# The FFN down projection as seven block products instead of eight, with weight sums added up in DRAM

## The chip, the cores and the metric

The kernel runs on one core of a Trainium2 chip. A core has five engines with a queue of instructions each, taken in order: TensorE (PE in the rows, its weight loads PEld), VectorE (DVE), ScalarE (ACT), GpSimd (POOL) and SyncE (SP, which here only issues DMAs). They wait for one another through semaphores. DMAs are issued by SP, ACT and POOL and are carried out by 16 DMA engines. The metric is the device time of one execution, in microseconds (us), as the median of several runs.

## The reference

A decoder block on 512 tokens of width 1024, in float32: a gated linear recurrence and a sparse attention side by side, merged, and then a SwiGLU feed-forward block of width 2816. What the change touches is the last line but one:

```python
h = rms_norm(x, norm_ffn_pre[l])
f = (jax.nn.silu(h @ w_ffn_gate[l]) * (h @ w_ffn_up[l])) @ w_ffn_down[l]
x = x + rms_norm(f, norm_ffn_post[l])
```

Here `h` is 512 x 1024, the bracket (called `ff` below) is 512 x 2816, and `w_ffn_down` is 2816 x 1024.

## The kernel before

Every float32 product is made as three matmuls. An operand is split into a rounded part `hi` (written by ScalarE as a cast) and the rest `lo` (written by VectorE as source minus `hi`), and the product is hi x hi + hi x lo + lo x hi. `split` (L83 to L84) is that pair of instructions, and nearly every operand goes through it.

The stages in order of time: the input projections and the recurrence (to about 245 us), its output projection `rnn_out`, eight units of weights (to about 286), the attention, the merge and `w_o` (to about 540), the FFN's gate and up projections (`columns(m)`, 22 column blocks of 128, to 762), and the down projection with the last norm (762 to 889).

In the attention, 64 units (16 heads by 4 blocks of 128 queries) are run in an order written out by hand: `logits(u)` is made three units ahead (`AHEAD = 3`) of `probs(u)`, and between them run the matmuls of 13 further projections ("fill": queries, keys, gates), whose 512 KB weight tiles are loaded on POOL's queue (L220), multiplied by -1 on ScalarE (L246), and completed by a second, adding DMA on POOL's queue (L247), so that the tile holds `lo`. A query projection also needs a rotary step: ScalarE evacuates, VectorE shuffles (L478), POOL multiplies twice (L479, L480), VectorE adds (L481). TensorE's order is kept as written there; the other engines' orders are chosen by a scheduler when the program is built.

The gate and up projections already use seven block products with sums of blocks. For column block m, VectorE adds up weight blocks for block m + 1 (L971 to L974), splits them, and evacuates seven products (L1007 to L1013).

The down projection before is the plain one. For each of 22 row blocks k of 128, `load_d` brings 512 KB of weights, `prep_d` splits them, `prep_a` splits the matching pair of `ff` blocks every second time, and `down_mm` adds three matmuls (128 x 128 stationary, 512 columns moving) into each of eight PSUM banks, (q, c) for four blocks of 128 tokens and two halves of the output columns. For the last four k (`TAIL`), the order is bank by bank, so that `finish(q)` (the norm, the residual, the store) of one token block runs beside the matmuls of the next. `raw_tile`, `ws_tile` and the tag `tt` are small rotating sets of buffers.

## Time and profile before

| | |
|---|---|
| median of 3 runs | 892.28 us (889.8 to 892.52) |
| profiled execution | 890.67 us, of which the span of its instructions is 888.8 us and 1.87 us lie around it |
| TensorE, VectorE, ScalarE, GpSimd busy, share of the span | 96%, 70%, 56%, 26% |
| mean granted TensorE clock | 0.991 of full speed |

A busy share is a mean over all stages. Matmuls overlap one another in the pipeline: one lasts longer than the distance from its start to the next one's, so a stage's length is read from starts.

### The profile page before, as it was taken

Reading aid. Unit: us, or ns where it says so; the run is one execution under the profiler, and the core shown is the slowest. Engines: PE = TensorE matmul, PEld = TensorE weight load, DVE = VectorE, ACT = ScalarE, POOL = GpSimd, SP = SyncE. Lnnn points to the kernel's source line nnn. Section 1 sums busy time; section 2 is a strip of 40 time slices with the busy share of each in tenths; the row PEclk is TensorE's granted clock in tenths of the full one; section 3 lists DMA queues with packets and bytes.
Section 4 is the critical chain, followed back from the end, with each engine's and each line's share of the span. In section 5 each row is a group of like instructions: output and inputs, shape, how many; then the busy total and the mean of one; then the engine's idle time right before and its main releaser. Section 6 shows DMA issues by size and latency. Waiting matters only on the chain.

```text
span 888.8 us, 12985 instructions
## 1 busy us (share of the span) xinstructions
PE 857.5 (96%) x4811; PEld 740.9 (83%) x4811; DVE 620.6 (70%) x1109; ACT 494.7 (56%) x838; POOL 229.2 (26%) x242
## 2 busy tenths in 40 slices
PE   8999999999899989999999998999999999999996
PEld 5887888877688778888788887899999999888885
DVE  7686989976861687777466379888878887533415
ACT  5355457877430878777534356666656666323312
POOL 3262235453421432210022202233333332100000
PEclk9999999999899999999999999999999999999998
DMA  9488788758344745433445635778788878333104
GB/s 303 105 175 183 164 165 178 162 126 184 96 94 113 166 90 108 100 73 119 147 142 180 210 137 151 172 167 189 174 189 181 182 177 226 110 114 98 48 0 143
DMA packets 65697, 129.73 MB, mean 146 GB/s; under 512 B 8865, under 2 KB 32481, under 8 KB 65634
## 3 DMA queue, kind: packets, MB, share of 16 engines
q0 software_dynamic: 18432, 61.87, 35.6%
q1 hardware_dynamic: 46048, 64.92, 23.4%
q10 hardware_dynamic: 1154, 2.10, 0.6%
q8 instruction: 38, 0.62, 0.3%
q14 instruction: 25, 0.20, 0.1%
HBM read 122.59 MB, written 6.29 MB: 145 GB/s over the span
## 4 chain that ended last, share of the span: by engine, by line
PE 62%; DVE 13%; DMA 8%; issue 8%; ACT 7%; POOL 2%; SPq 0%; DVEq 0%; ACTq 0%; POOLq 0%
PE acc L286 6%; PE acc L284 6%; PE acc L288 6%; PE bank L990 5%; DMA ws<-in_t_ff_dram 5%; PE bank L988 4%; PE bank L989 4%; PE bank L1064 3%; PE bank L1062 3%; PE bank L1063 3%; PE ps_o L742 2%; PE ps_t L732 2%; DVE xc L584 2%; PE acc L990 1%; PE acc L988 1%
## 5 line engine op out<-in xcount | busy, mean ns | idle before, releaser
L84 DVE TENSOR_TENSOR ws<-raw,ws 128x1024 fp32r<-128x1024 f32 x44 | 61.0, 1390 | 66.2 <-ACT ws L84 66.2
L284 PE MATMUL acc<-hT,ws 128*128 128x512 f32 x248 | 98.7, 398 | 1.4 <-ACT xpad L580 1.4
L286 PE MATMUL acc<-hT,ws 128*128 128x512 f32 x248 | 99.0, 399 | 0.0
L288 PE MATMUL acc<-hT,ws 128*128 128x512 f32 x248 | 98.7, 398 | 0.0
L84 ACT CAST ws<-raw 128x1024 fp32r<-128x1024 f32 x44 | 46.1, 1052 | 71.0 <-PE bank L1064 37.5
L982 POOL DMA_DIRECT2D ws<-in_t_ff_dram x40 | 35.2, 881 | 157.6 <-ACT ws L981 88.6
L84 ACT CAST ws<-sums 128x1024 fp32r<-128x1024 f32 x40 | 40.1, 1048 | 52.6 <-DVE sums L972 51.7
L990 PE MATMUL bank<-T,ws 128*128 128x256 f32 x200 | 57.8, 290 | 2.0 <-DMA ws<-in_t_ff_dram 1.7
L988 PE MATMUL bank<-T,ws 128*128 128x256 f32 x200 | 56.5, 283 | 1.1 <-ACT ws L84 1.1
L284 PEld LDWEIGHTS acc<-hT,ws 128*128 128x128 f32 x248 | 46.7, 188 | 11.8 <-ACT xpad L580 1.9
L989 PE MATMUL bank<-T,ws 128*128 128x256 f32 x200 | 56.4, 282 | 0.0
L989 PE MATMUL bank<-B,ws 128*128 128x256 f32 x200 | 56.3, 282 | 0.0
L988 PE MATMUL bank<-B,ws 128*128 128x256 f32 x200 | 56.1, 281 | 0.0
L990 PE MATMUL bank<-B,ws 128*128 128x256 f32 x200 | 55.9, 280 | 0.0
L286 PEld LDWEIGHTS acc<-hT,ws 128*128 128x128 f32 x248 | 46.7, 188 | 10.0
L288 PEld LDWEIGHTS acc<-hT,ws 128*128 128x128 f32 x248 | 46.7, 188 | 9.8
L84 DVE TENSOR_TENSOR ws<-sums,ws 128x1024 fp32r<-128x1024 f32 x40 | 48.0, 1238 | 7.5 <-ACT ws L84 7.5
L284 PE MATMUL acc<-hT,raw 128*128 128x512 f32 x120 | 48.0, 400 | 1.2 <-ACT gl L572 1.2
L286 PE MATMUL acc<-hT,raw 128*128 128x512 f32 x120 | 48.1, 401 | 0.0
L288 PE MATMUL acc<-hT,raw 128*128 128x512 f32 x120 | 47.7, 398 | 0.0
L246 ACT ACTIVATE ws<-ws 128x1024 fp32r<-128x1024 f32 x29 | 30.7, 1059 | 23.2 <-DMA ws<-in_t_in_dram 23.2
L973 POOL TENSOR_TENSOR sums<-raw 128x512 f32<-128x512 f32 x20 | 33.5, 1675 | 34.7 <-PE acc L990 10.8
(329 smaller groups left out, 2696.6 us busy)
## 6 DMA issues: line engine op xcount, KB each, us to landing
ws<-in_t_in_dram POOLq DMA_DIRECT2D x58, 512.0 KB, 5.6
raw<-in_t_ff_dram SPq DMA_DIRECT2D x40, 512.0 KB, 4.4
raw<-in_t_in_dram POOLq DMA_DIRECT2D x30, 512.0 KB, 5.6
raw<-in_w_ffn_down_dram SPq DMA_DIRECT2D x22, 512.0 KB, 3.7
ws<-in_t_ff_dram POOLq DMA_DIRECT2D x20, 512.0 KB, 5.7
ws<-in_t_ff_dram POOLq DMA_DIRECT2D x20, 256.0 KB, 6.9
raw<-in_w_rnn_out_dram SPq DMA_DIRECT2D x8, 512.0 KB, 4.2
raw<-in_w_att_out_dram SPq DMA_DIRECT2D x8, 512.0 KB, 4.1
```

The lines of the kernel that those rows point to most:

```text
L84: return SC.copy(hi, src).ins, (lo_engine or V).tensor_tensor(lo, src, f(hi), op=A.subtract).ins
L246: SC.mul(lo, f(hi), -1.0)
L284: pe(PE.matmul(ps, ws[0][:, k, :], hi(k), start=(n == 0), stop=False))
L286: pe(PE.matmul(ps, ws[0][:, k, :], lo(k), start=False, stop=False))
L288: pe(PE.matmul(ps, ws[1][:, k, :], hi(k), start=False, stop=(n == len(order) - 1)))
L973: G.tensor_tensor(s3, a11, a21, op=A.subtract)
L982: G.dma_start(dst[:, 1], t_ff[n, m].rearrange("p (k c) -> p k c", c=P)[:, k], accum_op=A.add)
L988: PE.matmul(ps, a[:, 0, k, :], b[:, 0, k, :], start=(k == 0), stop=False)
L989: PE.matmul(ps, a[:, 0, k, :], b[:, 1, k, :], start=False, stop=False)
L990: PE.matmul(ps, a[:, 1, k, :], b[:, 0, k, :], start=False, stop=(k == 3))
L1062: PE.matmul(ps, a[:, 0, ts], b[:, 0, cs], start=(k == 0), stop=False)
L1063: PE.matmul(ps, a[:, 0, ts], b[:, 1, cs], start=False, stop=False)
```

## The change

The down projection `ff @ w_ffn_down` is written as a 2 x 2 block product and made with seven block products instead of eight. The blocks of `ff` are two halves of the tokens (256 each) by even and odd row blocks; those of the weights are even and odd row blocks by two halves of the output columns (512). With four sums of weight blocks (U1 to U4) and three sums of `ff` blocks, the products are P1 to P7. Each product has 11 steps j (one per pair of row blocks), two token blocks t and three matmuls per step.

The weight sums are made in DRAM. Two new inputs hold copies of weight blocks in another order (`t_dn`, `t_dn2`). `down_sums(n)`, called at two places in `rnn_out`'s loop and at five in the attention, issues for a group of three j (11 j in four groups): first a 1 MB copy within DRAM on SP's queue, at the next call a 512 KB adding DMA on POOL's queue, and at the two calls after that a 256 KB adding DMA each. That is 11 copies on SP's queue and 33 adding DMAs on POOL's, all with source and target in DRAM.

The down projection then has two phases. In the first, P6, P5, P7 and P4 run together over j with the summed weights (1 MB per j): `prep_d` splits them and `prep_a` makes the three `ff` sums on VectorE and splits these and two blocks. In the second, P1, P3 and P2 run one after the other, with weight blocks loaded from `w_ffn_down` itself and `ff` blocks split again (`prep_l`). Then the results are added up on VectorE, and `finish` follows; for the last product the first token block's matmuls stand ahead of the second's (`TAIL = 6` steps).

```diff
+    def down_sums(n):
+        for step, g in enumerate(range(n, n - 4, -1)):
+            for j in range(GROUP * g, min(GROUP * g + GROUP, NJ)) if g >= 0 else ():
+                u = u_dram[j]
+                with tc.issue_after(after["pool"]), tc.issue_after(after["sp"]):
+                    if step == 0:
+                        ld(u, t_dn[j])
+                    elif step == 1:
+                        G.dma_start(u[:, 0:2], t_dn2[j], accum_op=A.add)
+                    else:
+                        G.dma_start(u[:, step:step + 1], u[:, 2 * step - 4:2 * step - 3], accum_op=A.add)
...
         rnn_out(m)
         drain(4)
+        if m in (1, 5):
+            down_sums(m // 4)
...
             values(u // NT - 1)
+            if u // NT % 3 == 2:
+                down_sums(2 + u // NT // 3)
...
+    def prep_d(j):
+        x, z = ws_tile(0, [P, 2, 2, 512]), ws_tile(1, [P, 2, 2, 512])
+        for raw, w in zip(raw_d.pop(j), (x, z)):
+            split(raw, w[:, 0], w[:, 1])
...
+    def prep_a(j):
+        ff = ff_pair(j)
+        a11, a12, a21, a22 = ff[:, 0, 1], ff[:, 1, 1], ff[:, 0, 0], ff[:, 1, 0]
+        sa = ffp.tile([P, 2, H], F32, name="sa", tag="u", bufs=2)
+        V.tensor_tensor(sa[:, 0], a22, a21, op=A.subtract)
+        V.tensor_tensor(sa[:, 1], a11, a21, op=A.subtract)
+        V.scalar_tensor_tensor(a21, sa[:, 0], -1.0, a11, op0=A.mult, op1=A.subtract)
+        t = ws_tile(0, [P, 2, 4, H]) if j == 0 else ffp.tile([P, 2, 4, H], F32R, name="as", tag="tt", bufs=4)
+        split(sa, t[:, 0, 0:2], t[:, 1, 0:2])
+        split(ff[:, :, 0], t[:, 0, 2:4], t[:, 1, 2:4])
...
-    for k in range(FT):
-        if k + 2 < FT:
-            load_d(k + 2)
...
+    for j in range(NJ):
+        if j + 2 < NJ:
+            load_d(j + 2)
+        if j + 1 < NJ:
+            prep_d(j + 1)
+            prep_a(j + 1)
+        wd, ad = ws_d.pop(j), as_d.pop(j)
+        for t in range(2):
+            for n, a, b in (("P6", "S2", "U2"), ("P5", "R1", "U1"), ("P7", "S3", "U3"), ("P4", "A22", "U4")):
+                down_mm(pq[n, t], t, ad[a], wd[b], j == 0, j == NJ - 1)
...
+    jobs = [("P1", 0, 0), ("P3", 1, 1), ("P2", 1, 0)]
+    steps = [(n, e, c, j0) for n, e, c in jobs for j0 in range(0, NJ, 2)]
...
+    for t in range(2):
+        p6, p5, p7, p4 = (pq[n, t] for n in ("P6", "P5", "P7", "P4"))
+        V.tensor_copy(xb[:, 0, t], p6)
+        V.tensor_tensor(xb[:, 1, t], p5, xb[:, 0, t], op=A.add)
+        V.tensor_tensor(xb[:, 0, t], p7, xb[:, 0, t], op=A.add)
+        V.tensor_tensor(xa[:, 1, t], p5, xb[:, 0, t], op=A.add)
+        V.tensor_tensor(xa[:, 0, t], p4, xb[:, 0, t], op=A.add)
...
+    for t in range(2):
+        for i in range(len(steps) - TAIL, len(steps)):
+            step_mm(i, t)
+        V.tensor_tensor(xb[:, 0, t], pl["P2", t], xb[:, 0, t], op=A.add)
+        finish(t, [xb[:, 0, t], xb[:, 1, t]])
```

In the rows below, lines of the change are those of the changed kernel: `split`'s VectorE half is L85 there, loads of fill weights L221, their adding DMAs L248, the rotary products L480 and L481.

First place, POOL's queue in the attention, from the load of one fill weight to the next rotary step. In the kernel before:

```order
L220 DMA ws_3333<-in_t_in_dram 128x1024
L247 DMA raw_3077<-in_t_in_dram 128x1024
L220 DMA raw_3459<-in_t_in_dram 128x1024
L479 TENSOR_TENSOR rp_x_3446<-rp_x_3446,rope_c_131 128x512
L480 TENSOR_TENSOR rp_s_3447<-rp_s_3447,rope_s_132 128x512
```

and in the changed one, of the same stretch, up to the second load (L694 is the 512 KB addition, L696 the 256 KB ones):

```order
L221 DMA ws_3373<-in_t_in_dram 128x1024
L694 DMA u_dram9_1977<-in_t_dn2_dram 128x1024
L694 DMA u_dram10_1978<-in_t_dn2_dram 128x1024
L696 DMA u_dram6_1974<-u_dram6_1974 128x512
L696 DMA u_dram7_1975<-u_dram7_1975 128x512
L696 DMA u_dram8_1976<-u_dram8_1976 128x512
L696 DMA u_dram3_1971<-u_dram3_1971 128x512
L696 DMA u_dram4_1972<-u_dram4_1972 128x512
L696 DMA u_dram5_1973<-u_dram5_1973 128x512
L248 DMA raw_3106<-in_t_in_dram 128x1024
L221 DMA raw_3507<-in_t_in_dram 128x1024
```

Eight adding DMAs now stand between the two loads, and five more (two for group 3, three for group 2) between the second load and the same rotary step. Each DMA on this queue is issued only once the eighth DMA before it on the queue has landed, since they share eight semaphores in turn. The longest row of additions, nine, stands one fill unit earlier.

Second place, VectorE at the end of the gate and up projections. `o`, `u` and `ff<-o` are evacuations of `columns`; `ws<-raw` splits down weights, `sa` and `as` are sums of `ff` blocks and their splits. In the kernel before, between the evacuation of the last but one column block and the last one's:

```order
L1013 TENSOR_TENSOR ff<-o 128x512
L84 TENSOR_TENSOR ws<-raw,ws 128x1024 x2
L1007 TENSOR_TENSOR u<-u 128x256
L1008 TENSOR_TENSOR o<-acc,u 128x512
L1009 TENSOR_TENSOR o<-acc,o 128x256
L84 TENSOR_TENSOR ws<-ff,ws 128x1024
```

and in the changed one, from the same evacuation:

```order
L1035 TENSOR_TENSOR ff<-o 128x512
L85 TENSOR_TENSOR ws<-raw,ws 128x1024 x2
L1090 TENSOR_TENSOR sa<-ff 128x256
L1091 TENSOR_TENSOR sa<-ff 128x256
L1029 TENSOR_TENSOR u<-u 128x256
L1092 SCALAR_TENSOR_TENSOR ff<-sa,ff 128x256
L1030 TENSOR_TENSOR o<-acc,u 128x512
L85 TENSOR_TENSOR ws<-raw,ws 128x1024
L1032 TENSOR_TENSOR o<-bank_7653,u 128x256
L85 TENSOR_TENSOR as<-sa,as 128x512
L1031 TENSOR_TENSOR o<-acc,o 128x256
```

The sums and splits for the first steps of the down projection are interleaved with the last evacuations.

Third place, VectorE at the very end of the changed kernel: `acc_8592` is P2 of the first token block and `acc_8651` that of the second, L1221 adds them, L884 multiplies by the norm's gain, L888 makes the output rows.

```order
L1221 TENSOR_TENSOR xb_8207<-acc_8592,xb_8207 128x512
L884 TENSOR_TENSOR rest_8631<-xb_8207,xc_8208 128x512
L96 TENSOR_SCALAR rs_v_8639<-ss2_8632 128x1
L884 TENSOR_TENSOR rest_8690<-xb_8207,xc_8208 128x512
L99 RECIPROCAL rs_r_8641<-rs_r_8641 128x1
...
L888 SCALAR_TENSOR_TENSOR rest_8631<-rest_8631,rs_r_8641,x1_8629 128x512
L888 SCALAR_TENSOR_TENSOR rest_8631<-rest_8631,rs_r_8641,x1_8627 128x512
L1221 TENSOR_TENSOR xb_8207<-acc_8651,xb_8207 128x512
L884 TENSOR_TENSOR rest_8690<-xb_8207,xc_8208 128x512
```

The addition for the second token block stands behind the first block's whole norm. On TensorE, the scheduler mixes the two blocks' matmuls: 17 of them come after the first block's last one.

## Rows read from the trace of the kernel before

**Rows 1.** The page: part 1, TensorE to GpSimd; part 2, the granted clock.
```profile
PE 857.5 (96%) x4811; PEld 740.9 (83%) x4811; DVE 620.6 (70%) x1109; ACT 494.7 (56%) x838; POOL 229.2 (26%) x242
...
PEclk9999999999899999999999999999999999999998
```

**Rows 2.** Windows: stretch, its length, busy us (x instructions) of PE, PEld, DVE, ACT, POOL, clock, DMA share, GB/s.
```profile
744.50:762.00 17.50, 17.50 (x148) 17.49 (x148) 10.88 (x15) 9.55 (x12) 1.77 (x2) 1.00 0.86 248
762.00:881.80 119.80, 119.73 (x529) 98.79 (x527) 45.35 (x56) 34.52 (x46) 3.16 (x1) 1.00 0.25 78
881.80:888.80 7.00, 0.00 (x0) 0.00 (x0) 2.77 (x7) 0.89 (x3) 0.00 (x0) 0.64 0.20 76
```

**Rows 3.** Timeline of TensorE (start, duration): first and last down matmul; a fill's start.
```profile
294.21 0.48 PE L284 MATMUL acc<-hT,raw 128*128 128x512 f32 x1
...
761.87 0.39 PE L1062 MATMUL bank<-ws 128*128 128x512 f32 x1
...
881.35 0.39 PE L1064 MATMUL bank<-wt,ws 128*128 128x512 f32 x1
```

**Rows 4.** Groups, 762 to 889 us: busy us, mean ns, idle before it and its releaser.
```profile
L84 DVE TENSOR_TENSOR ws<-raw,ws 128x1024 fp32r<-128x1024 f32 x14 | 17.0, 1223 | 37.9 <-ACT ws L84 37.9
L84 ACT CAST ws<-raw 128x1024 fp32r<-128x1024 f32 x14 | 14.6, 1053 | 40.7 <-PE bank L1064 37.5 <-issue 3.2
...
L866 DVE SCALAR_TENSOR_TENSOR rest<-rest,rs_r,x 128x512 f32<-128x512 f32 x8 | 5.7, 749 | 0.1
...
L862 DVE TENSOR_TENSOR rest<-bank,gfin 128x512 f32<-128x512 f32 x6 | 4.1, 689 | 17.1 <-ACT u L109 17.1
```

**Rows 5.** Timeline of VectorE in the evacuation of a column block.
```profile
742.07 0.41 DVE L1010 TENSOR_TENSOR o<-bank,u 128x256 f32<-128x256 f32 x1
742.39 0.68 DVE L1011 TENSOR_TENSOR o<-bank,o 128x512 f32<-128x512 f32 x1
743.77 0.69 DVE L1013 TENSOR_TENSOR ff<-o 128x512 f32<-128x512 f32 x1 [0.70 <-ACT o L1012]
```

**Rows 6.** Timeline at the end: norm of the third and the last token block.
```profile
876.39 0.60 ACT L109 ACTIVATE u<-acc 128x512 f32<-128x512 f32 x1 [2.03 <-PE acc L1064]
...
878.84 1.42 DVE L866 SCALAR_TENSOR_TENSOR rest<-rest,rs_r,x 128x512 f32<-128x512 f32 x2
...
881.83 0.60 ACT L109 ACTIVATE u<-bank 128x512 f32<-128x512 f32 x1 [2.03 <-PE bank L1064]
...
882.55 0.69 DVE L862 TENSOR_TENSOR rest<-bank,gfin 128x512 f32<-128x512 f32 x1 [1.69 <-ACT u L109]
...
884.28 1.42 DVE L866 SCALAR_TENSOR_TENSOR rest<-rest,rs_r,x 128x512 f32<-128x512 f32 x2
```

**Rows 7.** Windows, the attention, columns as in rows 2.
```profile
300.00:400.00 100.00, 97.19 (x541) 83.15 (x540) 79.04 (x205) 80.54 (x195) 27.43 (x29) 1.00 0.48 97
```

**Rows 8.** Timeline of GpSimd, fill weights and a rotary step.
```profile
254.89 0.59 POOL L220 DMA_DIRECT2D raw<-in_t_in_dram  x1 [7.17 <-DVE ws L84]
...
359.70 0.55 POOL L220 DMA_DIRECT2D ws<-in_t_in_dram  x1 [7.47 <-PE acc L288]
...
371.91 1.29 POOL L479 TENSOR_TENSOR rp_x<-rp_x,rope_c 128x512 f32<-128x512 f32 x1 [1.54 <-DVE rp_s L478]
```

**Rows 9.** The page: part 3 (packets, MB, share of 16 engines), part 6 (us to landing).
```profile
q1 hardware_dynamic: 46048, 64.92, 23.4%
...
ws<-in_t_ff_dram POOLq DMA_DIRECT2D x20, 512.0 KB, 5.7
ws<-in_t_ff_dram POOLq DMA_DIRECT2D x20, 256.0 KB, 6.9
```

**Rows 10.** Timeline of VectorE in the attention: the same unit of two heads.
```profile
374.03 0.42 DVE L716 CUSTOM_DVE_ANT_0 sm<-ps_s,mask 128x256 f32<-128x256 f32 x1
...
382.30 0.42 DVE L716 CUSTOM_DVE_ANT_0 sm<-ps_s,mask 128x256 f32<-128x256 f32 x1 [0.59 <-PE ps_s L711]
```

**Rows 11.** Timeline of SyncE's queue: the last five loads for `rnn_out`.
```profile
224.66 24.53 SPq L230 DMA_DIRECT2D raw<-in_w_rnn_out_dram  x5
```

More of the change, by code (lines that the diff above doesn't have):

```diff
@@ L36 @@
 PLAIN = 2
-TAIL = 4
+TAIL = 6
 START = 24
@@ L229, in do_load @@
         if kind == "c":
-            ld(raw, w[:, where:where + P].rearrange("(k p) c -> p k c", p=P))
+            after["sp"] = ld(raw, w[:, where:where + P].rearrange("(k p) c -> p k c", p=P)).ins
         else:
@@ L678, in hybrid_block @@
     gb_dram = dram.tile([KT, P, S], F32, name="gb_dram")
+    NJ = FT // 2
+    u_dram = [dram.tile([P, 4, 512], F32, name=f"u_dram{j}") for j in range(NJ)]
+    def down_sums(n):
[9 more added lines that the diff above has]
+                        G.dma_start(u[:, step:step + 1], u[:, 2 * step - 4:2 * step - 3], accum_op=A.add)
     def gate_b(m):
@@ L1055, in prep_a, with load_d @@
-    def prep_a(j):
-        as_d[j] = ws_tile(1, [P, 2, 2 * S])
-        split(ff_pair(j).rearrange("p e n c -> p (e n c)"), as_d[j][:, 0], as_d[j][:, 1])
-    def down_mm(ps, k, q, c):
-        a, b = as_d[k // 2], ws_d[k]
-        ts, cs = slice(k % 2 * S + q * P, k % 2 * S + (q + 1) * P), slice(c * 512, (c + 1) * 512)
-        PE.matmul(ps, a[:, 0, ts], b[:, 0, cs], start=(k == 0), stop=False)
-        PE.matmul(ps, a[:, 0, ts], b[:, 1, cs], start=False, stop=False)
-        PE.matmul(ps, a[:, 1, ts], b[:, 0, cs], start=False, stop=(k == FT - 1))
+    def load_d(j):
+        raw_d[j] = []
+        for c in range(2):
+            t = raw_tile(c, [P, 2, 512])
+            ld(t, u_dram[j][:, 2 * c:2 * c + 2, :])
+            raw_d[j].append(t)
@@ L1066, in hybrid_block, with down_mm @@
+    def down_mm(ps, t, a, b, first, last):
+        ts = slice(t * P, (t + 1) * P)
+        PE.matmul(ps, a[:, 0, ts], b[:, 0], start=first, stop=False)
+        PE.matmul(ps, a[:, 0, ts], b[:, 1], start=False, stop=False)
+        PE.matmul(ps, a[:, 1, ts], b[:, 0], start=False, stop=last)
+    NJ = FT // 2
     for m in range(PLAIN, FT):
@@ new lines, in hybrid_block, with load_l, prep_l @@
+    raw_l, ws_l, as_l = {}, {}, {}
+    def load_l(i):
+        n, e, c, j0 = steps[i]
+        w = min(2, NJ - j0)
+        raw_l[i] = raw_tile(i % 2, [P, 2, 512])
+        ld(raw_l[i][:, 0:w], w_dn[e][:, j0:j0 + w, c * 512:(c + 1) * 512])
+    def prep_l(i):
+        n, e, c, j0 = steps[i]
+        w = min(2, NJ - j0)
+        x = ws_tile(i % 2, [P, 2, 2, 512])
+        raw = raw_l.pop(i)
+        split(raw[:, 0:w], x[:, 0, 0:w], x[:, 1, 0:w])
+        if i % 2 == 0:
+            as_l[i] = ffp.tile([P, 2, 4, H], F32R, name="al", tag="tt", bufs=4)
+        t = as_l[i - i % 2][:, :, i % 2 * 2:i % 2 * 2 + 2]
+        for q in range(w):
+            ff = ff_pair(j0 + q)
+            a = {"P1": ff[:, 0, 1], "P2": ff[:, 1, 1], "P3": ff[:, 0, 0]}[n]
+            if n == "P3":
+                V.scalar_tensor_tensor(a, ff[:, 1, 1], -1.0, a, op0=A.mult, op1=A.subtract)
+            split(a, t[:, 0, q], t[:, 1, q])
+        ws_l[i] = x, t
@@ L1086, in finish @@
+    for i in range(2):
+        load_l(i)
+    prep_l(0)
+    for t in range(2):
[5 more added lines that the diff above has]
+        V.tensor_tensor(xa[:, 0, t], p4, xb[:, 0, t], op=A.add)
+    def finish(t, cs):
         base = []
@@ L1117, in hybrid_block, with step_mm @@
-    for q in range(NT):
-        for c in range(2):
-            for k in range(FT - TAIL, FT):
-                down_mm(pd[q, c], k, q, c)
-        finish(q)
+    pl = {}
+    def step_mm(i, t):
+        n, e, c, j0 = steps[i]
+        if j0 == 0:
+            pl[n, t] = acc() if n == "P2" else bank4()
+        for q in range(min(2, NJ - j0)):
+            down_mm(pl[n, t], t, ws_l[i][1][:, :, q], ws_l[i][0][:, :, q], j0 + q == 0, j0 + q == NJ - 1)
+    for i, (n, e, c, j0) in enumerate(steps):
+        if i + 2 < len(steps):
+            load_l(i + 2)
+        if i + 1 < len(steps):
+            prep_l(i + 1)
+        if i < len(steps) - TAIL:
+            for t in range(2):
+                step_mm(i, t)
+        if j0 + 2 >= NJ and n == "P1":
+            for t in range(2):
+                SC.copy(xb[:, 0, t], pl["P1", t])
+                V.tensor_tensor(xb[:, 1, t], pl["P1", t], xb[:, 1, t], op=A.add)
+                for q in range(2):
+                    V.tensor_tensor(xa[:, q, t], xa[:, q, t], xb[:, 0, t], op=A.add)
+            for t in range(2):
+                finish(t + 2, [xa[:, 0, t], xa[:, 1, t]])
+        if j0 + 2 >= NJ and n == "P3":
+            for t in range(2):
+                V.tensor_tensor(xb[:, 1, t], pl["P3", t], xb[:, 1, t], op=A.add)
@@ L1166 @@
     named.append(("t_ff", _np.stack([_tiled(inputs[n], range(0, D_FF, P)) for n in ("w_ffn_gate", "w_ffn_up")])))
+    dn = _np.asarray(inputs["w_ffn_down"])[0].reshape(FT // 2, 2, P, 2, 512).transpose(0, 2, 1, 3, 4)
+    blocks = {f"{e + 1}{c + 1}": dn[:, :, e, c] for e in range(2) for c in range(2)}
+    named.append(("t_dn", _np.stack([blocks[n] for n in ("11", "22", "22", "21")], axis=2)))
+    named.append(("t_dn2", _np.stack([blocks["12"], blocks["12"]], axis=2)))
     for name, a in named:
```

56 lines of the change are left out of this document (21 added, 35 removed).

## The prediction

> **What bounds the kernel now.** I read the page first: TensorE is busy for 96% of the span and its clock stays at the upper level, 2.4 GHz, nearly throughout [rows 1]. Then the windows: from 762 to 881.8 us, the down projection, TensorE is busy all the time (119.73 of 119.80), while VectorE works 45 us, ScalarE 35 and the DMA engines are 25% busy [rows 2]. So this stage is bound by the number of matmuls alone, and a matmul less is time less, as long as the other engines keep up. What one costs is not its 0.39 us. The stage's first matmul starts at 761.87 and its last at 881.35 [rows 3], and there are 528 (22 k, 8 banks, 3 each; the window counts 529 with one of the stage before): 119.48 / 527 = 0.2267 us from start to start. After the last, 7 us follow in which TensorE is idle.
>
> **What is removed.** Seven products of 11 j, 2 t and 3 matmuls are 462, all with 512 columns as before: 66 fewer. 66 x 0.2267 = 15.0 us, which the change can gain and not more.
>
> **VectorE in the down projection.** This is where the cover is thin. Before, it had 22 weight splits and 11 `ff` splits; now it has 37 splits of 128x1024 or the like, sums, second splits of `ff`, and additions of products. From the evacuation that ends at 743.77 + 0.69 = 744.5 [rows 5], counted along the order to the last weight split of the last step, there stand 37 instructions of 1024 elements, 53 of 512, 83 of 256 and 6 tiny ones (six evacuations of 512 and six of 256 of the last two column blocks among them). By durations of 1.22, 0.69, 0.42 and 0.2 us [rows 4, 5] that is 45.1 + 36.6 + 34.9 + 1.2 = 117.8 us. But instructions that don't wait start before the one ahead has ended: 742.07 to 742.39 is 0.32, where the duration is 0.41 [rows 5]. At 0.08 less for each of 173 it is 104 us. TensorE reaches that split's product at its 444th matmul, 761.87 + 443 x 0.2267 = 862.3, so VectorE has 117.8 us for it. By durations the room is zero, by starts it is 13.8 us, a load of 88%. The room can't be used freely: the buffers let VectorE run about three steps ahead in the first phase, where a step costs it 2 x 1.14 + 2 x 0.61 + 4 x 0.34 = 4.9 us against TensorE's 24 x 0.2267 = 5.4; and each `lo` waits for ScalarE's cast, which comes in ScalarE's own order. ScalarE itself has 37 casts of 1.05 us [rows 4] and 58 shorter ones, some 65 us in all, and is not the bound. I take a loss of **2.5 us** of TensorE's time, mainly in the first steps, nearer the lower end, because back-to-back starts are what the rows show of a full VectorE; the bounds are 0 and some 12 (the rival below).
>
> **Loads in the down projection.** 1 MB per step of 5.4 us, then 0.5 MB per 2.7 us: about 193 GB/s, against 78 now. In the last columns 248 GB/s were moved with TensorE never idle [rows 2]. I cost it at nothing; if that cover fails, each load late by 1 us costs up to 1 us in a step.
>
> **The tail.** The last token block now needs one more addition (0.69 us) ahead of its norm. The multiplication with the gain stood behind ScalarE's square, 882.55 against 881.83 [rows 6], and reads another buffer now, which can give 0.7 back. But VectorE's second L1221 stands behind the whole norm of the first block. That norm took 876.39 to 878.84 + 1.42 = 880.26, 3.9 us [rows 6]; with an addition ahead it is 4.6, and only 17 x 0.2267 = 3.85 us of matmuls lie between the two blocks' ends. So the addition is late by about 0.7. Sum **0.7 us** lost; bounds 0 and 1.4.
>
> **The additions in the attention.** TensorE lost 2.8 of 100 us there, but VectorE and ScalarE are 80% busy, and the DMA engines 48% [rows 7]. Added are 33 adding DMAs (11.5 MB) in POOL's queue and 11 copies (11.5 MB) in SP's. TensorE sees none of them unless something queued behind on POOL is late: a fill's weights, or a rotary step, for which VectorE's next instruction waits and behind that VectorE's whole attention. The row that bears on this is a 512 KB addition that lands 5.7 us after its issue, with a 256 KB one issued behind it landing after 6.9 [rows 9]. Issued some 0.6 apart (an issue takes 0.55 to 0.59 [rows 8]), the second adds 6.9 + 0.6 - 5.7 = 1.8 us, so 3.5 for 512 KB; both are into SBUF, and none within DRAM was run. In the worst place, the eight additions behind the load of 359.70, the last of the five DMAs ahead of the rotary step waits for the seventh addition to land: 360.3 + 5.7 + 3.5 + 5 x 1.8 = 378.5, and the step starts near 379 where it started at 371.91 [rows 8], 7 us late. Cover: logits run three units ahead, a unit takes (382.30 - 374.03) / 4 = 2.07 us [rows 10], so 6.2 us. What is left is 1 us there, less elsewhere. Bounds: 0, and 19 at twice that time per byte. I take **2 us**, since additions within DRAM read both operands there.
>
> A rule of the Trainium skill (page "DMA: Bandwidth & Descriptors", section "Anatomy of one DMA — SWDGE (gpsimd) path") gives 2.0 us plus the bytes at 436 GB/s, so by estimate 3.2 us for 512 KB and 7.4 us for the first seven additions together; by it the rotary step would not be late at all, and the sum below would be 2 us lower. The row shows 5.7 us for the first of them, beside other traffic, and the row is what I use.
>
> **The sum**, made against the profiled execution's own 890.67 us (888.8 span and 1.87 around it): 15.0 - 2.5 - 0.7 - 2 = 9.8 us, 880.9. The median of the runs stands 1.6 us above that execution, so I put the forecast a little higher: **881.5 us**.
>
> **Rivals.** *VectorE sets the pace.* For it: by durations there is no room at all. Against it: starts. If the mean instruction costs its full duration and a tenth more goes in waits for casts and buffers, 117.8 x 1.1 = 129.6 and the last split's product moves from 862.3 to 874.1: 11.8 us lost instead of 2.5, and a time of 890.67 - 15.0 + 11.8 + 0.7 = 888 with the attention undisturbed (885 to 891 as waits go).
>
> *GpSimd's queue stalls the attention*, the other sign. Mechanism: additions within DRAM are so much slower than those into SBUF that the rotary step behind eight plus five of them is late beyond its cover. At x times the row's time the step is 7 + (x - 1) x 18.2 us late, and the loss is that less 6.2. The change's other terms leave 11.8; to end 2.7 us above the old time the loss must be 14.5, so x = 1.75. At x = 2 the loss is 19 and the time about 898. For it: both operands in DRAM, 2 KB rows, up to nine in a row. Against it: the DMA engines are half idle, and little else moves in this stretch (97 GB/s [rows 7]).
>
> *The copies delay weights.* The copies are 16 pieces of 64 KB. SP has nothing else to do from 249.2, the end of its `rnn_out` loads [rows 11], so six copies of 1 MB can go out at once. The plain queue took 23.4% of 888.8 us for 64.92 MB [rows 9], 3.2 us per MB: done by 268. The fill weight of 254.89 [rows 8], which landed and was completed in some 12 us, would then be ready at 281, before its use at 294.21 [rows 3]. At twice that time per MB it is 300, and 6 us are lost: 886.5. The skill's rule that an engine takes turns between queues packet by packet (same page, section "Queues, rings and completion order") is what would hold the small packets behind 64 KB pieces; no row here shows such pieces.
>
> **How the numbers follow.** 0.3% of 892.28 us, 2.7 us, is about what a measurement of this kernel can tell from no change: faster is below 889.6, slower above 895.0. The forecast has 0.64 (its own range 876 to 886), the pace of VectorE 0.17 (of it 0.05 within 0.3%), GpSimd's queue 0.13 (0.09 slower, 0.04 within), the copies 0.06 (0.01 within). That makes 0.81 faster, 0.10 same, 0.09 slower. The lower end, 876, is the full gain of 15.0 with no loss but part of the tail's; the upper, 890, takes in most of VectorE's case and the copies', and leaves out GpSimd's.
>
> **What would show it.** In the changed profile: 462 down matmuls 0.2267 us apart, clock at the upper level; TensorE's idle time between 762 and its end 0 to 5 us, released by VectorE's or ScalarE's splits; VectorE over 85% busy there; about 7.5 us after the last matmul; the attention as long as before within 3 us, and `rp_x` additions on VectorE not waiting for POOL by more than 1 us each. The forecast is wrong if TensorE's idle time in the down projection exceeds 8 us, or if the down projection starts over 8 us later than at 761.87, or if the first phase waits for loads of `u_dram`.

## The result: slower, 908.27 us

| | median us | over the kernel before, 95% interval |
|---|---|---|
| before | 891.99 | |
| after | 908.27 (905.68 to 910.28) | 1.0179 [1.0158, 1.0200] |

The profiled execution after took 908.55 us, its span is 906.75. The page after, parts 1 to 3 and 6 (answers to [rows 1, 9]):

```profile
PE 850.8 (94%) x4745; PEld 735.5 (81%) x4745; DVE 678.1 (75%) x1235; ACT 524.1 (58%) x902; POOL 259.5 (29%) x276
...
PEclk9999999999899899799999999999999999999999
DMA  8488888759599797998354563667787878847623
...
q0 software_dynamic: 23184, 73.41, 42.3%
q1 hardware_dynamic: 50912, 85.11, 29.2%
...
u_dram<-in_t_dn_dram POOLq DMA_DIRECT2D x11, 512.0 KB, 13.3
u_dram<-u_dram POOLq DMA_DIRECT2D x22, 256.0 KB, 13.2
```

TensorE does less, but its clock line has new dents (slices 14 and 17 of 40), and they lie in the attention, where the DMA line shows 7s and 9s instead of 3s to 7s. The additions landed 13 us after their issue, where [rows 9] had 5.7 and 6.9.

Windows cut where a stage's first matmul starts: first the kernel before, from the first matmul of `rnn_out` to the first one of the attention's output projection (columns as in rows 2):

```profile
240.10:432.30 192.20, 188.31 (x975) 158.98 (x976) 125.52 (x301) 123.06 (x281) 44.35 (x46) 0.99 0.45 102
```

and after: the same stretch, from there to the down projection, the down projection, and the tail:

```profile
241.80:463.00 221.20, 195.07 (x977) 164.78 (x977) 126.16 (x301) 123.42 (x281) 72.32 (x79) 0.93 0.80 179
463.00:793.68 330.68, 322.60 (x2292) 302.13 (x2290) 253.05 (x354) 191.04 (x278) 85.62 (x70) 0.99 0.71 179
793.68:898.30 104.62, 104.62 (x464) 86.55 (x462) 98.36 (x174) 62.33 (x109) 3.64 (x2) 1.00 0.53 170
898.30:906.80 8.50, 0.28 (x2) 0.00 (x0) 4.63 (x10) 0.93 (x3) 0.00 (x0) 0.77 0.32 123
```

So the time is accounted for, in spans:

| stretch | before | after | |
|---|---|---|---|
| start to the first `rnn_out` matmul | 240.1 | 241.8 | +1.7 |
| `rnn_out` and attention | 192.2 | 221.2 | **+29.0** |
| merge, `w_o`, gate and up | 329.5 | 330.7 | +1.1 |
| first to last down matmul | 119.48 | 104.52 | **-14.96** |
| last down matmul to the end | 7.45 | 8.56 | +1.1 |
| span | 888.80 | 906.75 | +17.95 |

The down projection gave what it was to give. The attention took it twice over: TensorE idled 221.2 - 195.1 = 26.1 us there instead of 3.9, and its busy time grew by 6.8 us because the granted clock was 0.93 instead of 0.99. Four of its waits there are longer than 1.5 us: 7.2, 3.3, 11.8 and 3.3. Who it waited for, after (us in total, times, longest):

```profile
PE ps_t L752 <- DVE pt L85: 18.7, 5, 11.8
PE acc L289 <- DMA ws<-in_t_in_dram: 7.2, 1, 7.2
```

The 11.8 us is in GpSimd's timeline: the burst of nine additions, behind it a fill weight's addition (L248) and the rotary step (L480), and VectorE's addition that waited for that step:

```profile
350.66 2.58 POOL L694 DMA_DIRECT2D u_dram<-in_t_dn_dram  x3
352.30 4.32 POOL L696 DMA_DIRECT2D u_dram<-u_dram  x4
366.47 0.82 POOL L696 DMA_DIRECT2D u_dram<-u_dram  x1 [9.85 <-issue]
371.89 0.81 POOL L696 DMA_DIRECT2D u_dram<-u_dram  x1 [4.59 <-DMA u_dram<-in_t_dn_dram]
374.81 0.90 POOL L248 DMA_DIRECT2D ws<-in_t_in_dram  x1 [2.11 <-DMA u_dram<-in_t_dn_dram]
376.40 0.57 POOL L221 DMA_DIRECT2D ws<-in_t_in_dram  x1 [0.69 <-issue]
376.98 1.28 POOL L480 TENSOR_TENSOR rp_x<-rp_x,rope_c 128x512 f32<-128x512 f32 x1
...
379.51 0.69 DVE L482 TENSOR_TENSOR rp_x<-rp_x,rp_s 128x512 f32<-128x512 f32 x1 [13.38 <-POOL rp_s L481]
```

Seven additions go out in 5 us. The eighth and ninth wait until earlier transfers of the queue have landed, and the rotary step waits with them, up to 376.98. The queue held back sooner than its eight semaphores ask for: the eighth addition goes out just after the first has landed (366.2), although the eighth transfer before it, the load of 350.07, had landed at 354.6. In e3 below, which moves instead of adding, the eighth goes out at 351.5, without such a wait. Why is not shown. VectorE stands still for 13.4 us, for a step that is only queued late.

The 7.2 us is earlier, and TensorE's timeline shows the clock's part too:

```profile
289.18 0.40 PE L287 MATMUL acc<-hT,ws 128*128 128x512 f32 x1
296.82 0.79 PE L289 MATMUL acc<-hT,ws 128*128 128x512 f32 x1 [7.24 <-DMA ws<-in_t_in_dram]
297.41 0.63 PE L285 MATMUL acc<-hT,ws 128*128 128x512 f32 x1
```

The matmul after the wait takes 0.79 us, twice the 0.40 of the one before: TensorE is back at the lower of its two levels, 1.2 GHz. What was late is a weight's addition behind the first burst, and that burst itself came late: behind the six copies at 251, of which the profile (issues from 250 to 276 us after: size, median us to landing) shows

```profile
raw<-in_t_in_dram POOLq DMA_DIRECT2D x3, 512.0 KB, 11.4
...
u_dram<-in_t_dn_dram SPq DMA_DIRECT2D x6, 15.5
```

two of the three fill transfers beside them needed 11.4 us or more; in the kernel before such a load took 5.1.

The two waits of 3.3 us differ. The one that ends at 410.85 is behind a later row of additions, the place that the prediction had priced. In the one that ends at 333.43 VectorE itself waited for nobody: one of its instructions, which takes 0.69 us elsewhere in the attention, took 2.91.

```profile
327.72 2.91 DVE L488 TENSOR_TENSOR qst<-rp_x,qst 64x512 fp32r<-64x512 f32 x1
```

It ran beside GpSimd's two rotary products (327.2 to 330.1). In e4, where VectorE makes these products, it never took longer than 0.69 in the attention. That GpSimd held it up fits this, but no run tests it alone.

### The profile page after: what moved, and what is told of

The parts are those of the page before. It is cut to its first block, busy times and chain, and to the rows that moved or that the text cites. A ratio compares the mean times of both kernels' runs of the same rounds, so it can differ in the third digit from the quotient of the medians.

```text
span 906.8 us, 13184 instructions
## 1 busy us (share of the span) xinstructions
PE 850.8 (94%) x4745; PEld 735.5 (81%) x4745; DVE 678.1 (75%) x1235; ACT 524.1 (58%) x902; POOL 259.5 (29%) x276
## 4 chain that ended last, share of the span: by engine, by line
PE 53%; DVE 14%; DMA 12%; issue 9%; ACT 6%; POOL 4%; SPq 1%; DVEq 0%; ACTq 0%; POOLq 0%
PE acc L285 6%; PE acc L287 6%; PE acc L289 6%; DMA ws<-in_t_ff_dram 5%; PE bank L1012 5%; PE bank L1010 4%; PE bank L1011 4%; PE bank L1102 2%; PE bank L1100 2%; PE bank L1101 2%; DVE xc L585 2%; PE acc L1010 2%; PE acc L1011 1%; PE acc L1012 1%; DMA ws<-in_t_in_dram 1%
## 5 line engine op out<-in xcount | busy, mean ns | idle before, releaser
L289 PE MATMUL acc<-hT,ws 128*128 128x512 f32 x248 | 99.8, 403 | 7.2 <-DMA ws<-in_t_in_dram 7.2
L85 DVE TENSOR_TENSOR ws<-raw,ws 128x1024 fp32r<-128x1024 f32 (+1 forms) x66 | 85.7, 1308 | 26.9 <-ACT ws L85 26.9
L285 PE MATMUL acc<-hT,ws 128*128 128x512 f32 x248 | 99.9, 403 | 1.4 <-ACT xpad L581 1.4
L85 ACT CAST ws<-raw 128x1024 fp32r<-128x1024 f32 (+1 forms) x66 | 67.2, 1032 | 58.7 <-PE acc L289 20.2
L287 PE MATMUL acc<-hT,ws 128*128 128x512 f32 x248 | 100.0, 403 | 0.0
L85 ACT CAST ws<-sums 128x1024 fp32r<-128x1024 f32 x40 | 40.3, 1048 | 52.3 <-DVE sums L994 42.3
L289 PEld LDWEIGHTS acc<-hT,ws 128*128 128x128 f32 x248 | 47.5, 191 | 17.7 <-DMA ws<-in_t_in_dram 7.7
L1010 PE MATMUL bank<-T,ws 128*128 128x256 f32 x200 | 57.2, 286 | 2.5 <-ACT ws L85 2.5
L1012 PE MATMUL bank<-T,ws 128*128 128x256 f32 x200 | 58.7, 294 | 0.9 <-DMA ws<-in_t_ff_dram 0.6
L285 PEld LDWEIGHTS acc<-hT,ws 128*128 128x128 f32 x248 | 47.5, 192 | 12.0 <-ACT xpad L581 1.8
L1011 PE MATMUL bank<-T,ws 128*128 128x256 f32 x200 | 56.9, 285 | 0.0
L287 PEld LDWEIGHTS acc<-hT,ws 128*128 128x128 f32 x248 | 47.6, 192 | 10.1
L85 DVE TENSOR_TENSOR ws<-sums,ws 128x1024 fp32r<-128x1024 f32 x40 | 47.8, 1232 | 8.7 <-ACT ws L85 8.7
L736 DVE CUSTOM_DVE_ANT_0 sm<-ps_s,mask 128x256 f32<-128x256 f32 (+1 forms) x64 | 33.1, 521 | 26.1 <-PE ps_s L731 26.0
L752 PE MATMUL ps_t<-ident,sm 128*128 128x128 f32 x160 | 28.6, 277 | 18.7 <-DVE pt L85 18.7
```

Of the source, the lines that this page charges most:

```text
L85: return SC.copy(hi, src).ins, (lo_engine or V).tensor_tensor(lo, src, f(hi), op=A.subtract).ins
L285: pe(PE.matmul(ps, ws[0][:, k, :], hi(k), start=(n == 0), stop=False))
L287: pe(PE.matmul(ps, ws[0][:, k, :], lo(k), start=False, stop=False))
L289: pe(PE.matmul(ps, ws[1][:, k, :], hi(k), start=False, stop=(n == len(order) - 1)))
L736: V.tensor_tensor_reduce(sm[:, 0:n], ps[:, 0:n], masks[i], 1.0, -LOW, A.add, A.min, mn)
L752: pe(PE.transpose(pp[:, j * P:(j + 1) * P], sm[:, j * P:(j + 1) * P], ident))
```

## The experiments

Ratios are to the kernel before, run on the same chip.

| label | what | median us | ratio [95%] | attention us | from there to down us |
|---|---|---|---|---|---|
| e1_no_sums | 44 transfers left out | 878.24 | 0.9851 [0.9815, 0.9887] | 191.4 | 331.5 |
| e2_copies_only | 33 additions left out | 882.70 | 0.9888 [0.9853, 0.9924] | 193.4 | 335.7 |
| e3_plain_moves | moves for additions | 893.89 | 1.0025 [0.9999, 1.0050] | 210.8 | 328.9 |
| e4_rope_on_vector | rotary products on VectorE | 898.61 | 1.0071 [1.0045, 1.0096] | 211.0 | 330.4 |
| s2_by_fill | two additions at a time | 905.33 | 1.0142 [1.0116, 1.0168] | 217.4 | 331.8 |
| s4_in_merge | all additions in the merge | 919.91 | 1.0289 [1.0254, 1.0324] | 195.6 | 368.3 |
| s5_wide_rows | s2 with 4 KB rows for `w_att_out` | 886.36 | 0.9921 [0.9901, 0.9941] | 197.7 | 329.1 |
| s6_rest_in_ffn | s2, 15 additions in gate and up | 887.79 | 0.9943 [0.9925, 0.9961] | 192.6 | 335.7 |
| s7_together | spread over three stages, wide rows | 886.83 | 0.9942 [0.9924, 0.9961] | 193.2 | 337.9 |
| s8_ticked | held back by row sums, wide rows | 888.42 | 0.9957 [0.9940, 0.9973] | 204.0 | 330.5 |
| b_wide_rows | kernel before with wide rows | 891.78 | 0.9996 [0.9982, 1.0011] | 192.9 | 331.1 |

The last two columns are starts of first matmuls in the profiled execution, as in the table above (before 192.2 and 329.5, after 221.2 and 330.7). In all ten runs with the seven products the down projection is 104.52 us from first to last matmul, without a gap.

**e1_no_sums**

```diff
-        if m in (1, 5):
-            down_sums(m // 4)
...
-            if u // NT % 3 == 2:
-                down_sums(2 + u // NT // 3)
...
-            ld(t, u_dram[j][:, 2 * c:2 * c + 2, :])
+            ld(t, t_dn[j][:, 2 * c:2 * c + 2, :])
```

> All 44 transfers that make the weight sums are left out; the down projection loads the unsummed blocks in their place, so it multiplies by blocks that are not sums. Theory (the whole loss comes from those transfers, the down projection itself gained what was forecast): the profile after shows the 462 matmuls without a gap and 8.6 us after the last one instead of 7.45, so 892.0 - 15.0 + 1.1 = 878, between 877 and 880, with the attention as in the kernel before. Rival (part of the 16 us is lost in the later stages, by VectorE or by the loads of the down projection): 885 or more.

878.24: the theory's number. The loss comes from the 44 transfers, and the rest of the change is worth 1.5%.

**e2_copies_only**

```diff
-                    elif step == 1:
-                        G.dma_start(u[:, 0:2], t_dn2[j], accum_op=A.add)
-                    else:
-                        G.dma_start(u[:, step:step + 1], u[:, 2 * step - 4:2 * step - 3], accum_op=A.add)
```

> The 11 copies stay where they are, the 33 additions are left out (so the blocks are not sums). Theory (it takes copies and additions together): the six copies at 251 make the fill load of 256.57 land about 12 us late and so the next loads are issued about 6 us late, but without the first three additions in front the addition that TensorE waited for lands in 5.6 us and not 13, at about 289.4, when it is wanted; nothing else waits. 878 to 881, no wait of TensorE for a weight above 2 us. Rival (the copies alone cost what the wait of 7.2 us and the lower clock behind it cost): 886 to 890.

882.70, between the two. The wait for the weight is 1.3 us, as the theory had it; the attention is 2 us longer than in e1, and 4 us more are lost in the gate and up stage, which holds none of these transfers. Those I can't assign to the copies; the intervals of e1 and e2 overlap.

**e3_plain_moves**

```diff
-                        G.dma_start(u[:, 0:2], t_dn2[j], accum_op=A.add)
+                        G.dma_start(u[:, 0:2], t_dn2[j])
...
-                        G.dma_start(u[:, step:step + 1], u[:, 2 * step - 4:2 * step - 3], accum_op=A.add)
+                        G.dma_start(u[:, step:step + 1], u[:, 2 * step - 4:2 * step - 3])
```

> The 33 transfers on GpSimd's queue stay, with the same sizes, sources and targets, but move their bytes without adding (so the blocks are not sums). Theory (the work of the DMA engines sets how late the burst is): if the adding is what makes a packet long, the nine of the long burst are through in about half the time, TensorE's 10.9 us of idleness between 360 and 380 shrink to a few us, and the time is 884 to 893. Rival (it is the number of transfers, eight in flight at a time and each with its own latency): the wait for the rotary step stays, 902 or more.

893.89, 0.9 above the theory's range, and the rival's 902 is not reached: same number, sizes and queue, 14 us less. What a byte costs is in the queue's row, first of the kernel before, then of e3:

```profile
q0 software_dynamic: 18432, 61.87, 35.6%
```

```profile
q0 software_dynamic: 21776, 73.41, 39.3%
```

11.5 MB more take 0.393 x 892.4 - 0.356 x 888.8 = 34 us of the 16 engines when they are moved, and 0.423 x 906.8 - 316 = 67 us when they are added: twice (with e2 as the base, 29 and 62). TensorE's longest wait fell from 11.8 to 6.1 us. But 18.6 of the attention's 29.0 us are there without any adding, and the wait for the weight is still 6.7 us. So the adding is one part of the loss, and the rest goes with the transfers themselves; whether with their number or their bytes e3 does not separate.

**e4_rope_on_vector**

```diff
+        R = V if state["ordered"] else G
-        G.tensor_tensor(xe, xe, rope_c, op=A.mult)
-        G.tensor_tensor(xs, xs, rope_s, op=A.mult)
+        R.tensor_tensor(xe, xe, rope_c, op=A.mult)
+        R.tensor_tensor(xs, xs, rope_s, op=A.mult)
```

> Everything is as in the changed kernel, the output too, but the two multiplications of the rotary step in the attention are made by VectorE instead of GpSimd. Theory (TensorE stands still because the rotary step stands behind the additions in GpSimd's queue): the wait between 360 and 380 and the smaller one near 405 vanish or shrink to a third, the 7.2 us for a weight near 290 stays; 7 steps of 1.4 us more on VectorE cost 0 to 4 us; 890 to 899. Rival (the DMA engines are full, so that fill weights are late whatever stands in the queue): TensorE waits for weights instead, 903 or more.

898.61, inside the theory's range, with every transfer still there. TensorE's waits in its attention:

```profile
PE acc L289 <- DMA ws<-in_t_in_dram: 11.1, 2, 8.4
PE ps_t L753 <- DVE pt L85: 6.9, 4, 5.1
```

The 11.8 us is gone; a fill weight, queued behind the same additions, is late by 2.7 us instead. So the order in GpSimd's queue is one cause, and not the only one: 5.1 us late in the attention stay, and I did not see then that they were of another kind (ScalarE waited 5.6 us for a load of `w_att_out` there).

**s2_by_fill.** `some(adds, n)` issues the next n additions, behind the last work that a projection puts into GpSimd's queue; the copies follow stores of gates (L703) on SyncE's.

```diff
+            some(adds, 2)
+            if kind == "g":
+                some(copies, 3)
```

> The same 44 transfers with the same sizes, the whole computation: two additions stand behind each of the 13 projections' last work on GpSimd's queue (18 in the attention), 15 stand behind the last weight's addition, and of the copies three are queued at 221, three at 251 and five behind later stores on SyncE's queue. Theory (it is what stands ahead of the rotary steps and weights in GpSimd's queue, and how much of it at once, not the bytes): two additions are some 4 us of the DMA engines, inside the cover of the logits; TensorE's extra idle time in the attention falls from 25 us to under 4, and the time is 878 to 883. Rival (the bytes are too many for the DMA engines in the attention wherever they stand): the loss falls by the 15 additions and five copies that are moved out at most, 890 or more.

905.33: my theory, as it then stood, failed, and the number is the rival's. But the loss has moved. Windows of it:

```profile
340.00:360.00 20.00, 20.00 (x115) 17.26 (x114) 14.72 (x44) 15.52 (x39) 8.25 (x9) 1.00 1.02 291
...
400.00:420.00 20.00, 13.05 (x75) 11.12 (x73) 6.18 (x18) 5.40 (x15) 3.91 (x5) 0.91 1.06 187
420.00:440.00 20.00, 4.42 (x13) 3.21 (x14) 4.62 (x9) 6.54 (x14) 4.26 (x6) 0.50 0.85 172
```

Up to 394 us, 18 additions and the last five copies cost TensorE nothing, with the DMA engines full: it waited 2.2 us for VectorE up to there, and 2.4 in the kernel before. That is against the rival's mechanism. The changed kernel had issued 18 additions by 372 too, and idled 7.2 + 3.3 + 11.8 us in three waits around them. All of s2's loss is at the end, where no fill weight is left to hold GpSimd back and 15 additions go out in a row. Who waited there is neither a rotary step nor a fill weight, but ScalarE, and issues from 400 to 425 us show for what (queues, then us to landing):

```profile
424.46 1.04 ACT L85 CAST ws<-raw 128x1024 fp32r<-128x1024 f32 x1 [17.25 <-DMA raw<-in_w_att_out_dram]
```

```profile
q0 software_dynamic: 1427, 3.89, 89.7%
q1 hardware_dynamic: 1851, 1.04, 17.1%
...
raw<-in_w_att_out_dram SPq DMA_DIRECT2D x2, 512.0 KB, 28.1
```

SyncE's load of the next stage's weights, 4.3 us in the kernel before, took 28. ScalarE's cast of it stands in the same queue as the exponentials of the attention, and they stood behind it. The load's rows are 512 bytes, 1024 packets; while it ran, the two queues got packets through in like numbers (1427 and 1851), and a packet of the additions costs far more (0.897 x 25 x 16 / 1427 = 0.25 us against 0.04). The Trainium skill (page "DMA: Bandwidth & Descriptors", section "Queues, rings and completion order") says that an engine goes round its queues, a packet at a time. The trace agrees as far as these counts go, and it is the rule that I had weighed in the third rival the other way round, for large packets ahead of small ones.

**s4_in_merge**

```diff
+        after["pool"] = G.tensor_tensor(gb[m], gb[m], ma[m], op=A.add).ins
+        some(adds, 5)
```

> As the kernel before this one, but all 33 additions stand in the merge behind the attention, about five behind each of its eight additions on GpSimd. Theory: no rotary step and no fill weight stands behind them, so the attention is that of the kernel with copies alone less its early wait, 878 to 882; what can be late is the merge's addition on GpSimd (a block's is due 5.4 us after the one ahead, five additions within DRAM take some 9 us of the DMA engines, but eight may be in flight), which the output projection would wait for with up to 8 us in all. Rival (whatever GpSimd has to do behind such a row of transfers is late): 886 to 890, with the wait in the merge. Rival (bytes): the DMA engines are full from 445 to 510 and the weights of the output projection are late, 884 or more.

919.91: worse than each case. The attention is nearly free of loss (195.6), and the merge and `w_o` take 38 us more, where both mechanisms meet. Its waits from 440 to 540 us:

```profile
ACT mg L85 <- POOL gb L825: 50.4, 7, 11.8
...
PE bank L872 <- ACT mg L85: 14.4, 3, 7.2
ACT gb L818 <- DMA gb<-gb_dram: 13.7, 5, 8.9
```

GpSimd's own addition of the merge stood behind five transfers, and the loads of `gb` came late besides.

**s5_wide_rows** tests the packets: s2, and only the layout of `w_att_out` in DRAM is changed.

```diff
-    u_yb = [cols_unit(w_att_out, 0, m) for m in range(8)]
+    u_yb = []
+    for m in range(8):
+        units.append(("c", t_att[m], None, "s"))
+        u_yb.append(len(units) - 1)
```

> The additions stand as in the kernel with two behind each projection; changed is only how the eight weights of the attention's output projection lie in DRAM: as 4 KB rows (128 packets of 4 KB for 512 KB) instead of 512 byte rows (1024 packets). Theory (a DMA engine serves the loads' queue and the additions' queue packet by packet, so a load beside a row of additions takes its packets per engine times one addition's packet of 0.33 us: 64 packets are 23 us, as measured there, 8 packets are 4): the load of 401 lands in 4 to 7 us, ScalarE's cast of it no longer holds up the attention, the two waits of 14.2 and 8.4 us vanish or shrink below 4 us in all; 878 to 885. Rival (the engines are simply full between 394 and 436, and whatever comes behind the additions waits for the bytes ahead of it): the waits stay above 15 us, 898 or more.

886.36, 1.4 above the theory's range, and 19 us better by the row size of eight loads; the rival is out. Its two waits are 1.2 and 2.5 us instead of 14.2 and 8.4. Issues from 403 to 421 us:

```profile
raw<-in_t_att_dram SPq DMA_DIRECT2D x4, 512.0 KB, 11.2
```

11.2 us instead of 28.1. I had expected 4 to 7: the number of packets gives the direction, not the size. By the same section of the Trainium skill's page a packet in the turn is some 9 to 17 descriptors; if a row is one descriptor, a turn is longer than one addition's row. No run here shows whether that makes the size.

**b_wide_rows** makes the same edit, for `w_rnn_out` too, in the kernel before.

> The kernel before, without any of the change, but with the weights of both output projections as 4 KB rows. Theory (wide rows matter only beside the additions): the same as the kernel before within 0.3%, 890 to 894. Rival (the wide rows are a gain of their own, so that the 19 us between the two placements are not due to the additions): 885 or less.

0.9996: wide rows are worth nothing without the additions.

**s6_rest_in_ffn**

```diff
-            some(adds, 2)
+            some(adds, min(2, len(adds) - 15))
...
             prep_w(m + 1)
+            some(adds, 1)
```

> 18 additions two by two in the attention as before; the other 15 go one by one into the gate and up stage, each behind a column block's two weight additions on GpSimd's queue. Loads as in the change (512 byte rows). Theory (no run of additions meets a load of small packets or stands ahead of something that is waited for): the attention ends within 3 us of the kernel before; in the gate and up stage the DMA engines are 81% busy, 28 us of work over 135 us bring them near full, cost 0 to 4 us; 878 to 884. Rival (the DMA engines have no room in the gate and up stage): its weights come late, 888 or more.

887.79, nearer the rival. The attention is 192.6 us, so 18 additions and 11 copies cost it nothing; from there to the down projection it took 5 us more than the change. TensorE's waits for gate and up's weights in s6, in the kernel before, and in e2:

```profile
PE bank L1018 <- DMA ws<-in_t_ff_dram: 6.3, 9, 2.4
```

```profile
PE bank L990 <- DMA ws<-in_t_ff_dram: 1.7, 4, 0.8
```

```profile
PE bank L1008 <- DMA ws<-in_t_ff_dram: 4.8, 6, 1.7
```

e2 has no transfer of the sums in that stage, and its 335.7 us are the same as s6's. So it is not shown that the additions there cost the 5 us. And the profiled execution of s6 (883.24) is the fastest of its twelve, as that of s5 (883.85) is of its six: these two traces show less than the medians lost.

**s7_together** joins s6's placement (eight additions in the merge, seven in gate and up) with wide rows:

```diff
+        after["pool"] = G.tensor_tensor(gb[m], gb[m], ma[m], op=A.add).ins
+        some(adds, 1)
...
+        units.append(("c", t_rnn[m], None, "s"))
```

> All the lessons at once, whole computation: 18 additions two by two in the attention, eight one by one behind the merge's additions on GpSimd, seven in the gate and up stage, and the weights of both output projections (recurrence and attention) as 4 KB rows. Theory: what is left of the loss is the copies' and a little of the additions in the gate and up stage; 879 to 883, no wait of TensorE above 2 us that the kernel before does not have. Rival (each addition costs a share of the time by its bytes wherever it stands): the same 885 to 888 as the two kernels before this one.

886.83, the rival's number: no better than s5 or s6. The attention is nearly as in the kernel before; behind it 8.4 us are lost.

**s8_ticked** takes none in gate and up (eight stay in the merge), and lets GpSimd wait for a row sum before each three at the attention's end:

```diff
+            if h >= 9:
+                tick = small.tile([P, 2, NT], F32, name="tick")
+                after["pool"] = G.tensor_scalar(tick, r, 1.0, None, op0=A.mult).ins
+                some(adds, min(3, max(0, len(adds) - 8)))
```

> Whole computation. 16 additions two by two in the attention as before; 9 more in threes at the attention's end, each group held back by a tiny GpSimd instruction that reads a row sum of a later head, so that the queue cannot run ahead; 8 one by one in the merge; none in the gate and up stage; 4 KB rows for both output projections' weights. Theory (a run of additions costs only what is waited for behind or beside it, and the gate and up stage, 81% busy, had no room): the end of the attention loses under 2 us, the merge 2, the gate and up stage nothing; 881 to 885. Rival (about 8 us are lost by the 44 transfers wherever they stand): 886 to 888 again.

888.42, a miss, and again beside the rival's 886 to 888. Its merge and gate and up lost nothing (330.5 us), its attention 12. GpSimd's and ScalarE's rows:

```profile
398.85 2.57 POOL L697 DMA_DIRECT2D u_dram<-in_t_dn_dram  x3
...
415.61 1.04 ACT L85 CAST ws<-raw 128x1024 fp32r<-128x1024 f32 x1 [7.90 <-DMA raw<-in_t_att_dram]
```

Three 512 KB additions met the first loads of `w_att_out`, and even with wide rows ScalarE's cast was 7.9 us late.

## Why the prediction was wrong, step by step

**The gain**, 66 matmuls of 0.2267 us, 15.0: measured 14.96. The step's price from start to start is right, 104.52 / 461 = 0.2267.

**VectorE in the down projection**, 2.5 us lost: none. TensorE was busy for 104.62 of 104.62 us with VectorE at 98.36, 94%. The count by starts was the right one, and VectorE's waits for casts were small: its largest group there in the kernel after

```profile
L85 DVE TENSOR_TENSOR ws<-raw,ws 128x1024 fp32r<-128x1024 f32 x33 | 39.7, 1218 | 1.5 <-ACT ws L85 1.5
```

waited 1.5 us in all. The rival on VectorE's pace is out. **The loads** there cost TensorE nothing, as said; ScalarE waited 6.9 us for them in all.

**The tail**, 0.7 us: 8.56 - 7.45 = 1.1, inside its bounds (in the other ten runs with the seven products 0.4 to 1.0). The second L1221 did stand behind the first block's norm; it starts at 899.38, where the last matmul had started at 898.19:

```profile
898.05 1.42 DVE L888 SCALAR_TENSOR_TENSOR rest<-rest,rs_r,x 128x512 f32<-128x512 f32 x2
...
899.38 0.69 DVE L1221 TENSOR_TENSOR xb<-acc,xb 128x512 f32<-128x512 f32 x1
```

**The additions in the attention**, 2 us: measured 29.0, outside the bound of 19. This is the step that failed, and the range with it, since its upper end left this rival out. By bytes it was right: 11 x 3.5 + 22 x 1.8 = 78 us of the DMA engines were priced, 67 were measured, so the additions were cheaper than taken, x = 0.86 and not 1.75. It priced one place right: behind the load of 385.04 (359.70 in the kernel before) the rotary step started 21.7 us after the load instead of 12.2, so 9.5 us late where 7 were told, and TensorE waited 3.3 us where 1 was told.

```profile
385.04 0.56 POOL L221 DMA_DIRECT2D ws<-in_t_in_dram  x1 [4.73 <-PE acc L289]
...
406.70 1.56 POOL L480 TENSOR_TENSOR rp_x<-rp_x,rope_c 128x512 f32<-128x512 f32 x1
```

Four things in the step were wrong.
- *The place.* I priced the eight additions and five DMAs behind the load of 359.70 and called it the worst. The nine ahead of them are worse: two copies go out beside them, and the rotary step follows at once. My own formula, used there, gives some 364 for that step (the load of 350.07 is the queue's first of eight, and the step waits for the third addition: 350.7 + 5.7 + 2 x 3.5), 12 us later than the 351.5 that the kernel before would give it (there it starts 1.4 us after the load, rows below). It came at 376.98, 13 us later still, and the issue ahead of it followed the fourth addition's landing, since the queue held back at seven and not at eight.

```profile
347.47 0.55 POOL L220 DMA_DIRECT2D ws<-in_t_in_dram  x1 [7.26 <-PE acc L288]
348.86 1.29 POOL L479 TENSOR_TENSOR rp_x<-rp_x,rope_c 128x512 f32<-128x512 f32 x1 [0.84 <-DVE rsum L723]
```

- *The first landing.* This is most of the 13 us. I took 5.7 us for the first addition, from a row of additions that were not in a burst. Here it took 15.6 us, and the median of the three 512 KB ones is 20.4 (issues from 350 to 377 us after):

```profile
u_dram<-in_t_dn_dram POOLq DMA_DIRECT2D x3, 512.0 KB, 20.4
u_dram<-u_dram POOLq DMA_DIRECT2D x6, 256.0 KB, 24.1
```

  From the first landing to the third it took 8.3 us, where two times 3.5 were priced, so the time per byte was about right. Nor is it the adding that made the first one late: moves in its place (e3) took 13.7. Whether the two copies beside it did or the nine in flight at once, no run separates.
- *The cover was counted for rotary steps alone.* A fill weight's addition stood behind three additions that the six copies had made late, and cost 7.2 us. Copies and additions were two rivals of mine, with their chances apart; the copies by themselves give only 1.3 us (e2), and the additions by themselves were not run.
- *The clock was priced at nothing.* The long waits lowered it, and 6.8 us of the 29.0 are TensorE being busy for longer, at a granted clock of 0.93.

**The rivals.** "GpSimd's queue stalls the attention" is what happened, with a chance of 0.13; the mechanism and the wait's releaser are as told there, the longest wait is one burst earlier than told, and e4, which takes the rotary step out of that queue, removes the wait. Its condition, additions slower by 1.75 times, was not needed: at the place that it names, x came out as 1.1 (9.5 us late). What I missed besides is contention between queues, shown by s2 and s5. Of the signs that I had named, the down projection began 31.8 us later than at 761.87, and an `rp_x` addition waited 13.4 us for GpSimd; those for the down projection itself came as told. **The Trainium skill's rule** (page "DMA: Bandwidth & Descriptors", section "Anatomy of one DMA — SWDGE (gpsimd) path") of 2.0 us plus the bytes at 436 GB/s gives 3.2 us for the first addition, by estimate, and would have had no rotary step late. The trace does not agree in a burst (15.6); the row's 5.7 was nearer, and neither is a price for a burst.

**What stays open.** All versions with the sums that beat the kernel before lie at 886 to 888, and the transfers for nothing would be 878. Their waits (1 to 2 us near 295, then 3.7 in s5, 6.3 in s6, 7.3 in s8) explain a part of these 8 to 10 us, and the copies by themselves (e2) some 4. The rival of s7 and s8, that the 44 transfers cost about as much wherever they stand, forecast these numbers and is not ruled out; against it stands only that the loss lies elsewhere each time (5.5 and 11.8 us in the attention of s5 and s8, 6.2 and 8.4 behind it in s6 and s7). Some profiled executions, that of the change too, reach the first `rnn_out` matmul 1.5 to 2.4 us late. Most of that is there from 50 us on, long before the first copy is issued, and others don't have it; nothing here explains it.

## What to carry to other kernels

Transfers that nobody waits for still have a price, where they stand: count what is queued behind them on the issuing engine, and what is loaded beside them on other queues, and price the whole burst with the DMA engines' time of all that is in flight, not one transfer by itself. Two at a time behind the last urgent instruction cost nothing in the attention; nine ahead of one cost 12 us, and fifteen beside loads of 512 byte rows 22. Moving in place of adding took less than half of the loss away (14 of 30 us). A wait in a TensorE-bound stage cost more than its length here, since the clock was low behind it.

## What the runs showed of the hardware

Adding within DRAM took the DMA engines twice the time of moving the same bytes (67 against 34 us for 11.5 MB). But the first 512 KB transfer of a burst of nine beside two 1 MB copies landed after 15.6 us when it added and 13.7 when it moved, against 5.7 for additions into SBUF outside a burst. A load of 512 byte rows beside a run of additions took 28 us instead of 4.3, and 11 with 4 KB rows. From 300 to 380 us in s2 the DMA engines' share stood at 1.02 to 1.06, and up to 398 us TensorE waited no longer for VectorE than in the kernel before (2.2 us against 2.4). A run of additions on GpSimd's queue stopped at the eighth until the first had landed, a run of moves (e3) at the ninth. A VectorE instruction beside GpSimd's rotary products took 2.91 us instead of 0.69.
